# Gate sums kept plain until the branches read them, and several pieces of work in another order, in a one-core S5/attention/convolution layer

## The chip, the cores and the metric

One core of a Trainium2 chip runs the whole layer in one launch. The metric is the device time of one execution in microseconds (us). TensorE (PE) multiplies, VectorE (DVE), ScalarE (ACT) and GpSimd (POOL) do the elementwise work, SyncE (SP) issues nearly all transfers. Everything is float32; a matrix product is made of three matmuls on a split of each operand into a rounded part and a rest (hi·hi, hi·lo, lo·hi).

## What is computed

The layer, cut to what matters here (sequence 1024, width 1024, one layer):

```
proj = rms_norm(x, g1) @ w_in
u, q, k, v, cv, g = split(proj)                  # 512, 3x512, 512, 512, 1024, 3x1024 columns
y_s = GLU(gelu(S5(u)))                           # S5: 32 groups, a complex diagonal recurrence
y_a = dilated_attention(q, k, v) @ w_att_up      # three (window, dilation) patterns, merged by their log-sums
y_c = conformer_conv(cv) @ w_pw2                 # GLU, 31 taps per channel, layer norm, swish
gate = sigmoid(g + b_gate)                       # here as 0.5*(1+tanh(0.5*(g+b_gate)))
merged = gate[0]*y_s + gate[1]*y_a + gate[2]*y_c
x = x + merged @ w_out;  x = x + SwiGLU(rms_norm(x));  out = rms_norm(x)
```

## The kernel before

`run()` writes the program down stage by stage; a scheduler then orders each engine's instructions by their dependences and the places they were written at, and `tc.issue_after(x)` holds back what is written inside it until instruction x is issued. The engines then work strictly in that order. So where something is written, and in which queue a transfer stands, sets what waits behind it.

- **Start (0 to about 124 us).** `norm1` splits x into hi and lo; `conv_in(0)`, `project_v` and `project(0)` multiply it with columns of w_in (line L203 to L205 are the three matmuls of `gemms`). `conv(0)` is 31 steps on DVE into `cy` (L579). `s5_params` computes the recurrence's constants with many small DVE instructions, on tiles `sw`, `mr`, `pw`, `bb`; it is a generator in two parts, the first (some 100 instructions) written right after `project(0)`, the second in attention 0.
- **Attention (to about 547 us).** For each of 4 head pairs: `conv_in(hp+1)`, `attend0`, `attend1` (many small matmuls, a mask-and-minimum `soft` on DVE at L430, an exponential on ACT, transposes), `project(hp+1)`, `conv(hp)`. The evictions of `project` are on DVE (kn L417, q L417 and L424). The last head pair has no `project` of its own; instead `s5_tables` is written there: 44 DVE instructions twice over, which double a table `tab` of sines and cosines and store it.
- **Merge (547 to about 577 us).** `merge` weighs the results of `attend0` (first pattern, n0) and `attend1` (the other two, n1) (a chain PE, DVE, ACT, PE, ...: L515, L520, L525 to L534, L539, L546, L547) and stores the result (`od`, L550) from the SP queue.
- **Sides.** `project_u` multiplies for u (evicted by DVE to `uw`, L644). The gates use a seven-product scheme: two gates and two halves of the sequence take 7 products of half the depth instead of 8. Its right operands are seven sums of blocks of normed x: `early_sides` and `late_sides` load blocks `xb` (SP), scale them on DVE (`normed`, L662), add and split them (L675 to L693, L112). `first_products` runs the products that need early sides only: products 5 and 4 of gate pair 0, product 4 of pairs 1 and 2.
- **Gate stage (to about 924 us).** 12 pairs; `wino` runs the products in the order 1, 5, 2, 6, 4, 3, 7 through the PSUM banks u, y, v, z: products 1, 6 and 7 share bank u. After products 1, 5, 6, 4 ACT copies the bank to SBUF (`copy`, L710: m, y, n, z); after 2, 3, 7 DVE adds the other term (`add`, L716) and ACT takes the tanh in place (L717) and issues the store to DRAM `gd` (L718). Between products a `tick` hands out pieces of the eight S5 chunks (`s5`), one chunk every CHUNK = 8 products.
- **Branches (924 to 1156 us).** `gate(m, b)` loads a finished gate, two ahead of its use, from `gd`; DVE multiplies the branch's product by it. Then the output projection and the feed-forward part follow; the change does not touch them.

Of the kernel before, what the change touches and what calls it, by code (L numbers as in the profile page):

```python
# [9 lines left out]
F32 = mybir.dt.float32  # L10
# [19 lines left out]
CHUNK = 8  # L30
# [56 lines left out]
class Body:  # L87
# [158 lines left out]
    def run(self):  # L246
        tc, nc, V, A, G, PE = self.tc, self.nc, self.V, self.A, self.G, self.PE
        with ExitStack() as st:
# [8 lines left out]
            with pool("s5c") as self.sc, pool("h") as self.hp:  # L257
# [3 lines left out]
                with pool("at4") as self.ap4, pool("at1") as self.ap1, pool("at2") as self.ap2, pool("at3") as self.ap3, pool("at5") as self.ap5:  # L261
# [5 lines left out]
                    next(params)  # L267
                    for hp in range(HP):
                        if hp < HP - 1:
                            self.conv_in(hp + 1)  # L270
                        self.attend0(hp)
                        self.attend1(hp)
# [10 lines left out]
                early.close()  # L283
                self.bufs.update({"wraw": 6, "wsum": 3, "whi": 4, "wlo": 4, "t2": 8, "ct": 6, "l": 16, "r": 20})
                self.wp = enter(pool("w2", "right"))
                self.tp = right.enter_context(pool("t", "right"))
                with pool("xn") as self.xp, pool("uw") as self.up:
                    self.project_u()
                    begun = self.first_products()
                    for p in (1, 2, 3):  # L290
                        self.late_sides(p)
                with pool("s5") as self.sp:
                    self.gate_stage(begun)
# [109 lines left out]
    def project(self, hp):  # L403
# [15 lines left out]
        for a in (1, 2):  # L419
            q = self.ap2.tile([P, 4, 2, 2, 64], F32, tag=f"q{a}", name=f"q{a}")  # L420
            for h, ps in enumerate(self.gemm(win[4 + 4 * a + hp], self.hh, self.hl)):
                rb = perm(self.rb[:, 512 * h:512 * h + 512])
                for r in range(4):
                    V.tensor_tensor(out=q[:, r, :, :, 32 * h:32 * h + 32], in0=perm(ps)[:, r], in1=rb[:, r], op=ALU.mult)  # L424
            self.qkv.append(q)

    def soft(self, s, mask, c0, c1, pt, a, nm, den):

        w = self.ap2.tile([P, 320], F32, tag="sp", name="sp", bufs=2)
        self.V.tensor_tensor_reduce(out=w[:, c0:c1], in0=s[:, c0:c1], in1=mask[:, c0:c1], op0=ALU.add, op1=ALU.min,  # L430
                                    scale=1.0, scalar=3e38, accum_out=nm)
# [76 lines left out]
    def merge(self, half):  # L508
# [27 lines left out]
        for t in HALVES:  # L536
# [5 lines left out]
            for j in range(2):  # L542
# [7 lines left out]
                self.nc.sync.dma_start(out=self.od[hp][:, t], in_=self.n0[hp][:, t])  # L550
# [79 lines left out]
    def project_u(self):  # L630
        self.ud = self.dp.tile([L, 16, 32, NC], F32, name="ud")
        self.yd = self.dp.tile([BW, L, NC], F32, name="yd")
        self.kd = self.dp.tile([32, 16, KPAD + P], F32, name="kd")
        zero = self.tmp([P, 512])[:, 0:4 * KPAD].rearrange("p (a x) -> p a x", a=4)
        self.G.memset(zero, 0.0)
        self.nc.sync.dma_start(out=self.kd.rearrange("(a g) h x -> (g h) a x", a=4)[:, :, 0:KPAD], in_=zero)
        self.h1 = {}
        for ct in range(KB):
# [63 lines left out]
    def gate_pair(self, n, make, banks=None, only=PRODUCTS, kept=None):  # L702
# [26 lines left out]
    def first_products(self):  # L729

        self.gd = self.dp.tile([24, P, T], F32, name="gd")
        self.tick = lambda: None
        make = self.gate_left(0)
        begun = [(make, *self.gate_pair(0, make, only=(5, 4)), (1, 2, 6, 3, 7))]
# [681 lines left out]
```

## Time and profile before

| what | value |
|---|---|
| time, median of 3 runs (lowest to highest) | 1880.06 us (1879.17 to 1880.96) |
| the profiled execution's own time | 1877.27 us |
| its span in the trace | 1875.5 us |
| TensorE busy | 1777.2 us (95%) |
| mean granted TensorE clock | 0.963 of full speed |
| VectorE, ScalarE, GpSimd busy | 1303.8, 728.7, 865.9 us |

TensorE is busy for most of the span, but a matmul at a granted clock of 0.5 counts as busy for twice as long, so two things have to be read per stretch: the gaps of TensorE, and its clock.

### The profile page before, as it was taken

How to read it: one execution, taken by the hardware profiler on the slowest of the kernel's cores; microseconds unless marked ns; L12 is line 12 of the kernel's file. 1: busy time of each engine (PE TensorE's matmuls, PEld its weight loads, DVE VectorE, ACT ScalarE, POOL GpSimd, SP SyncE). 2: the span in 40 equal slices, each digit the busy share in tenths (PEclk: the TensorE clock that was granted, in tenths of full speed). 3: DMA queues.
4: the chain of work that ended last, by engine and by line, in shares of the span. 5: the costliest groups of instructions: out<-in, count | busy, mean ns of one | idle time of the engine just before them, and what ended most of it. 6: DMA issues, size and time to landing. Idle time of an engine off the chain costs nothing. (4 is left out here: it accounts for less than half of the span.)

```text
span 1875.5 us, 24385 instructions
## 1 busy us (share of the span) xinstructions
PE 1777.2 (95%) x8380; PEld 1392.3 (74%) x8380; DVE 1303.8 (70%) x2110; ACT 728.7 (39%) x1390; POOL 865.9 (46%) x707
## 2 busy tenths in 40 slices
PE   7989999999899689899999999989999999999997
PEld 5866675766657567788878878857888888778876
DVE  7964867746867987886467353698877776755556
ACT  5303314123141344445443233544555555433332
POOL 5622222222134665654325444665555445467671
PEclk9989999988888889999999999999999999999998
DMA  4430110210124534434752335313444444477752
GB/s 166 131 100 29 46 55 8 74 45 12 40 78 159 165 111 119 130 113 138 233 187 90 118 133 198 118 48 108 160 166 145 150 154 169 148 283 276 262 178 91
DMA packets 133516, 240.80 MB, mean 128 GB/s; under 512 B 13960, under 2 KB 55560, under 8 KB 133392
## 3 DMA queue, kind: packets, MB, share of 16 engines
q1 hardware_dynamic: 122576, 220.36, 34.9%
q10 hardware_dynamic: 10816, 18.88, 2.7%
q8 instruction: 66, 1.08, 0.2%
q14 instruction: 58, 0.48, 0.1%
HBM read 171.06 MB, written 68.12 MB: 128 GB/s over the span
## 5 line engine op out<-in xcount | busy, mean ns | idle before, releaser
L106 POOL TENSOR_TENSOR wlo<-wraw,whi 128x512 fp32r<-128x512 f32 x137 | 197.6, 1446 | 320.8 <-ACT whi L105 312.4
L112 POOL TENSOR_TENSOR wlo<-wsum,whi 128x512 fp32r<-128x512 f32 (+2 forms) x192 | 251.4, 1313 | 196.9 <-ACT whi L111 124.8
L112 POOL TENSOR_TENSOR wlo<-wraw,whi 128x512 fp32r<-128x512 f32 (+2 forms) x143 | 190.1, 1330 | 173.3 <-ACT whi L111 106.4
L167 PE MATMUL ps<-f,whi 128*128 128x512 f32 x616 | 241.7, 392 | 6.0 <-DVE f L112 4.0
L166 PE MATMUL ps<-f,whi 128*128 128x512 f32 x616 | 241.2, 392 | 5.3 <-ACT f L111 2.5
L105 ACT ACTIVATE whi<-wraw 128x512 fp32r<-128x512 f32 x135 | 84.6, 630 | 338.3 <-PE ps L204 225.7
L203 PE MATMUL ps<-hh,whi 128*128 128x512 f32 x448 | 186.6, 417 | 17.6 <-DVE kn L417 7.8
L204 PE MATMUL ps<-hl,whi 128*128 128x512 f32 x448 | 186.3, 417 | 4.1 <-DVE hl L349 4.1
L205 PE MATMUL ps<-hh,wlo 128*128 128x512 f32 x448 | 184.0, 411 | 0.0
L169 PE MATMUL ps<-f,wlo 128*128 128x512 f32 x616 | 165.5, 391 | 0.0
L166 PE MATMUL ps<-e,whi 128*128 128x512 f32 x336 | 138.8, 413 | 25.4 <-ACT n L710 10.0
L579 DVE SCALAR_TENSOR_TENSOR cy<-cx,hcw,cy 128x1024 f32<-128x1024 f32 x120 | 161.8, 1349 | 0.4
L111 ACT ACTIVATE whi<-wsum 128x512 fp32r<-128x512 f32 (+2 forms) x192 | 113.0, 592 | 119.2 <-PE ps L167 100.8
L167 PEld LDWEIGHTS ps<-f,whi 128*128 128x128 f32 x616 | 116.0, 188 | 33.9 <-DVE f L112 7.1
L166 PEld LDWEIGHTS ps<-f,whi 128*128 128x128 f32 x616 | 116.1, 188 | 32.0 <-ACT f L111 3.5
L167 PE MATMUL ps<-e,whi 128*128 128x512 f32 x336 | 135.7, 404 | 1.2 <-POOL e L112 1.2
L169 PEld LDWEIGHTS ps<-f,wlo 128*128 128x128 f32 x616 | 116.2, 189 | 24.2
L203 PEld LDWEIGHTS ps<-hh,whi 128*128 128x128 f32 x448 | 88.9, 198 | 42.8 <-issue 15.9
L111 ACT ACTIVATE whi<-wraw 128x512 fp32r<-128x512 f32 (+2 forms) x143 | 84.6, 592 | 87.0 <-PE ps L167 58.7
L166 PE MATMUL ps<-g,whi 128*128 128x512 f32 x280 | 109.5, 391 | 2.8 <-DMA g<-ad 2.7
L112 DVE TENSOR_TENSOR g<-ct,g 128x512 fp32r<-128x512 f32 x79 | 81.7, 1040 | 40.6 <-ACT g L111 40.4
L167 PE MATMUL ps<-g,whi 128*128 128x512 f32 x280 | 109.0, 389 | 0.0
(309 smaller groups left out, 3900.7 us busy)
## 6 DMA issues: line engine op xcount, KB each, us to landing
ad<-g SPq DMA_DIRECT2D x65, 512.0 KB
g<-ad SPq DMA_DIRECT2D x65, 512.0 KB
wraw<-in_win SPq DMA_DIRECT2D x122, 256.0 KB
wraw<-in_wffi SPq DMA_DIRECT2D x96, 256.0 KB
gate<-gd SPq DMA_DIRECT2D x24, 512.0 KB
wraw<-in_wffo SPq DMA_DIRECT2D x48, 192.0 KB
xb<-in_xt SPq DMA_DIRECT2D x32, 256.0 KB
wraw<-in_wout SPq DMA_DIRECT2D x32, 256.0 KB
```

The lines of the kernel that those rows point to most:

```text
L105: eng.tensor_copy(hi, raw) if eng else self.A.activation(hi, raw, AF.Copy)
L106: self.G.tensor_tensor(out=lo, in0=raw, in1=hi.bitcast(F32), op=ALU.subtract)
L111: self.A.activation(hi, src, AF.Copy)
L112: eng.tensor_tensor(out=lo, in0=src, in1=hi.bitcast(F32), op=ALU.subtract)
L166: PE.matmul(o, hi[:, k, :], xh, start=first and k == 0, stop=False, skip_group_check=not first)
L167: PE.matmul(o, hi[:, k, :], xl, start=False, stop=False, skip_group_check=not first)
L169: self.mm = PE.matmul(o, lo[:, k, :], xh, start=False, stop=k == n - 1, skip_group_check=not first).ins
L203: self.PE.matmul(o, hi[:, k, :], xh[k0 + k][:, t], start=first, stop=False)
L204: self.PE.matmul(o, hi[:, k, :], xl[k0 + k][:, t], start=False, stop=False)
L205: self.mm = self.PE.matmul(o, lo[:, k, :], xh[k0 + k][:, t], start=False, stop=last).ins
L579: V.scalar_tensor_tensor(out=cy, in0=cx[:, j:j + T], scalar=self.hcw[:, ct * TAPS + j:ct * TAPS + j + 1], in1=cy, op0=ALU.mult, op1=ALU.add)
```

## The change

What it does, by its parts:

1. After the DVE sums of the gate stage nothing follows on ACT. The plain sum is put on a list (`late`) and stored to `gd` from the SP queue two products later; `gate(m, b)` takes the tanh over 128x1024 after loading it.
2. `first_products` runs product 4 of pairs 1 to 5 (EARLY = 6), stores their copies to DRAM `zd` from SP, and `next_pair` loads them back.
3. The S5 chunks come every 7 products instead of 8, the first two pieces at products 9 and 12 instead of 4 and 7.
4. Part 1 of `s5_params` is written in attention 0, after the last q eviction of `project(0)`; part 2 stays where it was. The zero fill of `kd` moves to its end.
5. `s5_tables` may start only after the second `soft` of the last head pair's `attend0`.
6. The first three u weights are loaded ahead of the tables, the other five at the top of `project_u`.
7. The pool `at5` (v, kn, tables) is opened ahead of `at4`, so that the later `xb` tiles come to lie on other memory than n0 and n1 of the merge.
8. `merge` stores `od` from the POOL queue instead of SP's (4 stores in each of 2 merges).

The diff, cut to its core:

```diff
-CHUNK = 8
+CHUNK = 7
+EARLY = 6
...
-                with pool("at4") as self.ap4, pool("at1") as self.ap1, pool("at2") as self.ap2, pool("at3") as self.ap3, pool("at5") as self.ap5:
+                with pool("at5") as self.ap5, pool("at4") as self.ap4, pool("at1") as self.ap1, pool("at2") as self.ap2, pool("at3") as self.ap3:
...
                     params = self.s5_params()
-                    next(params)
+                    evicted = self.evicted
...
                         self.attend0(hp)
+                        soft = self.softs[1]
+                        if hp == 0:
+                            with tc.issue_after(evicted):
+                                next(params)
                         self.attend1(hp)
...
-                            self.s5_tables()
+                            self.first_u = [self.weights(self.i["win"][k // 2][:, 4 * (k % 2):4 * (k % 2) + 4], 4) for k in range(3)]
+                            with tc.issue_after(soft):
+                                self.s5_tables()
...
-                self.nc.sync.dma_start(out=self.od[hp][:, t], in_=self.n0[hp][:, t])
+                self.nc.gpsimd.dma_start(out=self.od[hp][:, t], in_=self.n0[hp][:, t])
...
+        self.ahead += [self.weights(self.i["win"][k // 2][:, 4 * (k % 2):4 * (k % 2) + 4], 4) for k in range(3, 8)]
...
                 V.tensor_tensor(out=x, in0=banks[b], in1=x, op=ALU.add)
-                A.activation(x, x, AF.Tanh, scale=0.5, bias=self.hbg[:, m:m + 1])
-                self.nc.scalar.dma_start(out=self.gd[m, :, HALVES[h]], in_=x)
+                self.late.append((self.ticks + 2, self.gd[m, :, HALVES[h]], x))
...
-        for n in (1, 2):
-            begun.append((None, *self.gate_pair(n, self.gate_left(n), only=(4,)), (1, 5, 2, 6, 3, 7)))
+        for n in range(1, EARLY):
+            r = self.gate_pair(n, self.gate_left(n), only=(4,))[1]
+            self.nc.sync.dma_start(out=self.zd[n], in_=r["z"])
...
+    def tick(self):
+
+        self.ticks += 1
+        while self.late and self.late[0][0] <= self.ticks:
+            _, dst, x = self.late.pop(0)
+            self.nc.sync.dma_start(out=dst, in_=x)
+        for part in self.parts.pop(self.ticks, ()):
+            with self.tc.issue_after(self.mm):
+                next(part)
...
+        elif n < EARLY:
+            z = self.tmp([P, 512], "z")
+            self.nc.sync.dma_start(out=z, in_=self.zd[n])
+            self.gate_pair(n, self.gate_left(n), None, (1, 5, 2, 6, 3, 7), {"z": z})
...
-        put(4, 0)
-        put(7, 0)
+        put(9, 0)
+        put(12, 0)
...
     def gate(self, m, b):
         t = self.tp.tile([P, 2, 512], F32, tag="t1", name="gate", bufs=4).rearrange("p a b -> p (a b)")
         self.nc.sync.dma_start(out=t, in_=self.gd[8 * b + m])
+        self.A.activation(t, t, AF.Tanh, scale=0.5, bias=self.hbg[:, 8 * b + m:8 * b + m + 1])
         return t
```

**DVE around the first key eviction.** `sw` is the parameters' scratch tile, `cy` the convolution's sum, `kn` the first eviction of `project(0)`. Before:

```order
L793 TENSOR_SCALAR sw_995<-sw_995 128x16
L846 TENSOR_SCALAR sw_995<-sw_995 128x16
L789 TENSOR_SCALAR sw_995<-sw_995 128x16
L790 TENSOR_SCALAR sw_995<-sw_995 128x16
L792 SCALAR_TENSOR_TENSOR sw_995<-sw_995 128x16 x3
L793 TENSOR_SCALAR sw_995<-sw_995 128x16
L417 SCALAR_TENSOR_TENSOR kn<-ps,rb 128x512 x2
L479 COPY kp<-kn 128x1024
```

In the changed kernel (lines have moved by 9 or 10: kn is L426):

```order
L576 TENSOR_TENSOR t_393<-ps,rb 128x512
L579 SCALAR_TENSOR_TENSOR t_393<-t_393,ps 128x512
L586 TENSOR_SCALAR cy<-cx_274,hcw,vecs 128x1024
L589 SCALAR_TENSOR_TENSOR cy<-cx_274,hcw,cy 128x1024 x30
L426 SCALAR_TENSOR_TENSOR kn<-ps,rb 128x512 x2
L489 COPY kp<-kn 128x1024
```

The parameter instructions that stood between the convolution and kn are gone from there.

**PE at the end of the last head pair's attention.** L203 to L205 before, L204 to L206 now, are the matmuls for u (`hh`, `hl` are the split normed x); L515 and L520 before, L525 and L530 now, are the first transposes of the merge. Before:

```order
L502 MATMUL ps<-ptT,v 64x128 x4
L438 MATMUL ps<-con,p 128x128 x4
L515 MATMUL ps<-con,stat 8x128 x8
L502 MATMUL ps<-ptT,v 64x128 x4
L438 MATMUL ps<-con,p 128x128 x4
L520 MATMUL ps<-con,r_4336 128x8 x8
L502 MATMUL ps<-ptT,v 64x128 x4
L539 MATMUL ps<-con,e 8x128 x4
L203 MATMUL ps<-hh_121,whi 128x512
L204 MATMUL ps<-hl_129,whi 128x512
L203 MATMUL ps<-hh_121,whi 128x512
```

In the changed kernel:

```order
L525 MATMUL ps<-con,stat 8x128 x4
L205 MATMUL ps<-hl_130,whi 128x512
L512 MATMUL ps<-ptT,v 64x128 x4
L448 MATMUL ps<-con,p 128x128
L525 MATMUL ps<-con,stat 8x128 x4
L206 MATMUL ps<-hh_122,wlo 128x512
L448 MATMUL ps<-con,p 128x128 x3
L204 MATMUL ps<-hh_123,whi 128x512
L530 MATMUL ps<-con,r_4358 128x8 x8
L205 MATMUL ps<-hl_131,whi 128x512
L206 MATMUL ps<-hh_123,wlo 128x512
L204 MATMUL ps<-hh_124,whi 128x512
```

The matmuls for u now stand ahead of and between the merge's transposes, where before the first of them came behind L539.

**ACT in the gate stage.** Copies of the banks (L710 before, L717 now), splits of the weights (`whi`), and before also tanh (L717) and stores (L718). Before:

```order
L710 ACTIVATE m<-ps 128x512
L111 ACTIVATE whi<-wsum 128x512
L111 ACTIVATE whi<-wraw 128x512
L946 ACTIVATE hs<-ca 64x2x128 x2
L717 ACTIVATE m<-m,hbg 128x512
L946 ACTIVATE hs<-ca 64x2x128 x2
L718 DMA gd<-m 128x512
L710 ACTIVATE n<-ps 128x512
L111 ACTIVATE whi<-wsum 128x512
L111 ACTIVATE whi<-wraw 128x512
L973 ACTIVATE gt<-ps 128x512
L717 ACTIVATE n<-n,hbg 128x512
```

In the changed kernel:

```order
L717 ACTIVATE m<-ps 128x512
L112 ACTIVATE whi<-wsum 128x512
L717 ACTIVATE y<-ps 128x512
L112 ACTIVATE whi<-wsum 128x512
L112 ACTIVATE whi<-wraw 128x512
L717 ACTIVATE n<-ps 128x512
L112 ACTIVATE whi<-wsum 128x512
L717 ACTIVATE z<-ps 128x512
L1054 ACTIVATE yg<-ps 128x512
L112 ACTIVATE whi<-wraw 128x512
L112 ACTIVATE whi<-wsum 128x512
```

No instruction is left on ACT that needs a DVE sum of the gates.

## Rows read from the trace of the kernel before

**Rows 1.** The page, busy time: each engine's busy us, share, instructions.

```profile
PE 1777.2 (95%) x8380; PEld 1392.3 (74%) x8380; DVE 1303.8 (70%) x2110; ACT 728.7 (39%) x1390; POOL 865.9 (46%) x707
```

**Rows 2.** Busy time by stretch (`us, PE busy (x) PEld busy (x) DVE busy (x) ACT busy (x) POOL busy (x), PEclk, DMA share, GB/s`).

```profile
459.00:503.00 44.00, 38.17 (x182) 30.57 (x181) 43.38 (x89) 3.10 (x6) 6.95 (x5) 0.95 0.10 36
503.00:547.00 44.00, 42.87 (x310) 25.82 (x310) 30.59 (x118) 24.39 (x76) 7.81 (x17) 0.89 0.09 37
547.00:579.00 32.00, 28.84 (x76) 16.01 (x77) 10.59 (x23) 4.84 (x9) 11.74 (x9) 0.57 0.41 129
579.00:640.00 61.00, 49.37 (x206) 39.41 (x205) 59.89 (x62) 19.70 (x34) 32.62 (x21) 0.93 0.56 177
640.00:700.00 60.00, 48.68 (x199) 37.36 (x200) 53.38 (x74) 22.58 (x43) 42.55 (x40) 0.84 0.37 124
700.00:924.00 224.00, 215.74 (x1116) 176.92 (x1116) 161.17 (x268) 109.71 (x195) 116.94 (x103) 0.99 0.44 136
924.00:1156.00 232.00, 229.98 (x1021) 188.39 (x1020) 122.82 (x174) 79.77 (x127) 100.58 (x74) 1.00 0.46 156
```

**Rows 3.** TensorE's timeline at 117 us: start, length, line, operation, [idle before <- releaser].

```profile
117.35 0.76 PE L203 MATMUL ps<-hh,whi 128*128 128x512 f32 x1 [7.76 <-DVE kn L417]
...
123.45 0.39 PE L205 MATMUL ps<-hh,wlo 128*128 128x512 f32 x1
```

**Rows 4.** Busy time of the `sw` tile's instructions alone, 43 to 117 us.

```profile
43.00:117.00 74.00, 32.51 (x99) 0.00 (x0) 0.97 0.39 120
```

**Rows 5.** Busy time by stretch, 182 to 215 us.

```profile
182.00:215.00 33.00, 31.74 (x226) 19.38 (x225) 23.22 (x50) 14.12 (x41) 10.46 (x17) 1.00 0.03 9
```

**Rows 6.** What TensorE waited for, 100 to 300 us: total, times, longest.

```profile
PE ps L203 <- DVE q L424: 2.5, 1, 2.5
```

**Rows 7.** TensorE's timeline where the last head pair's attention starts.

```profile
502.91 1.43 PE L459 MATMUL ps<-kn,q 64*128 64x256 f32 x4 [5.83 <-DVE stat L430]
```

**Rows 8.** Busy time of the `tab` tiles' instructions alone, in two stretches.

```profile
464.00:504.00 40.00, 14.19 (x44) 0.94 0.11 40
504.00:543.00 39.00, 11.49 (x44) 0.89 0.07 28
```

**Rows 9.** Groups of VectorE instructions, 545 to 650 us: busy, mean ns, idle before.

```profile
L662 DVE SCALAR_TENSOR_TENSOR xb<-xb,vecs,rb 128x512 f32<-128x512 f32 x32 | 34.5, 1113 | 0.7 <-DMA xb<-in_xt 0.7
...
L548 DVE TENSOR_TENSOR n<-n,ps 128x512 f32<-128x512 f32 x8 | 5.5, 688 | 12.1 <-PE ps L547 12.1
```

**Rows 10.** VectorE's timeline at 581 us.

```profile
581.15 0.75 DVE L662 SCALAR_TENSOR_TENSOR xb<-xb,vecs,rb 128x512 f32<-128x512 f32 x1 [0.71 <-DMA xb<-in_xt]
...
587.44 1.78 DVE L662 SCALAR_TENSOR_TENSOR xb<-xb,vecs,rb 128x512 f32<-128x512 f32 x1
```

**Rows 11.** GpSimd's timeline at 587 us.

```profile
586.99 1.68 POOL L112 TENSOR_TENSOR e<-xb,e 128x512 fp32r<-128x512 f32 x1 [3.22 <-ACT e L111]
```

**Rows 12.** What TensorE waited for in the gate stage, 600 to 925 us.

```profile
PE ps L166 <- ACT n L710: 10.0, 4, 5.0
...
PE ps L166 <- ACT m L710: 4.5, 3, 2.5
PE ps L166 <- ACT z L710: 3.9, 1, 3.9
```

**Rows 13.** Busy time by stretch, after the longest wait of the gate stage.

```profile
761.70:765.00 3.30, 3.30 (x8) 2.63 (x9) 1.23 (x1) 1.45 (x3) 3.27 (x3) 0.50 0.60 213
```

**Rows 14.** Line L717, the tanh of the gate sums: durations, and idle time before them.

```profile
L717 ACT ACTIVATE n<-n,hbg x12: 722/724/727, 668.8 to 921.9; 128x512 f32<-128x512 f32 x12
...
  DVE m L716: 51.0, 11
```

**Rows 15.** ScalarE's timeline at 759 us.

```profile
759.31 0.72 ACT L717 ACTIVATE m<-m,hbg 128x512 f32<-128x512 f32 x1 [8.04 <-DVE m L716]
...
761.05 0.58 ACT L710 ACTIVATE n<-ps 128x512 f32<-128x512 f32 x1
```

**Rows 16.** Groups of ScalarE instructions in the branches, 924 to 1156 us.

```profile
L105 ACT ACTIVATE whi<-wraw 128x512 fp32r<-128x512 f32 x49 | 30.5, 628 | 71.3 <-PE ps L204 41.2 <-issue 15.3 <-DMA cn<-cd 4.8
```

More of the change, by code (lines that the diff above doesn't have):

```diff
@@ L283, in run @@
                 early.close()
+                self.ahead = self.first_u
                 self.bufs.update({"wraw": 6, "wsum": 3, "whi": 4, "wlo": 4, "t2": 8, "ct": 6, "l": 16, "r": 20})
@@ L288, in run @@
                     self.project_u()
-                    begun = self.first_products()
+                    self.first_products()
                     for p in (1, 2, 3):
@@ L731, in first_products, with next_pair @@
         self.gd = self.dp.tile([24, P, T], F32, name="gd")
-        self.tick = lambda: None
+        self.zd = self.dp.tile([EARLY, P, 512], F32, name="zd")
+        self.late, self.ticks, self.parts = [], 0, {}
         make = self.gate_left(0)
-        begun = [(make, *self.gate_pair(0, make, only=(5, 4)), (1, 2, 6, 3, 7))]
-        for n in (1, 2):
-            begun.append((None, *self.gate_pair(n, self.gate_left(n), only=(4,)), (1, 5, 2, 6, 3, 7)))
+        self.begun = make, *self.gate_pair(0, make, only=(5, 4))
+        for n in range(1, EARLY):
+            r = self.gate_pair(n, self.gate_left(n), only=(4,))[1]
+            self.nc.sync.dma_start(out=self.zd[n], in_=r["z"])
         for p in (1, 2, 6):
             make(p, keep=True)
-        return begun
+    def tick(self):
[6 more added lines that the diff above has]
+                next(part)
+    def next_pair(self):
+        n = self.todo.pop(0)
+        if n == 0:
+            make, banks, r = self.begun
+            self.gate_pair(0, make, banks, (1, 2, 6, 3, 7), r)
+        elif n < EARLY:
+            z = self.tmp([P, 512], "z")
+            self.nc.sync.dma_start(out=z, in_=self.zd[n])
+            self.gate_pair(n, self.gate_left(n), None, (1, 5, 2, 6, 3, 7), {"z": z})
+        else:
+            self.gate_pair(n, self.gate_left(n))
     def toeplitz(self, g):
@@ L744, in toeplitz, with gate_stage @@
         return bass.AP(tensor=src.tensor, offset=src.offset, ap=[[16, L], [KPAD + P, 16], [1, P]])
-    def gate_stage(self, begun):
+    def gate_stage(self):
         n = 16 // NJ
-        parts = [self.s5(e) for e in range(n)]
-        at = {}
+        chunks = [self.s5(e) for e in range(n)]
         def put(t, e):
             if e < n:
-                at.setdefault(t, []).append(e)
-        put(4, 0)
-        put(7, 0)
+                self.parts.setdefault(self.ticks + t, []).append(chunks[e])
+        put(9, 0)
+        put(12, 0)
         for e in range(n):
-            t = 7 + CHUNK * e
+            t = 12 + CHUNK * e
             put(t + 3, e + 1)
@@ L764, in gate_stage @@
         for e in (0, 1):
-            next(parts[e])
-        self.ticks = 0
-        def tick():
-            self.ticks += 1
-            for e in at.pop(self.ticks, ()):
-                with self.tc.issue_after(self.mm):
-                    next(parts[e])
-        self.tick = tick
+            next(chunks[e])
         self.todo = list(range(len(GATES)))
-        while at:
-            g = self.todo.pop(0)
-            make, banks, r, only = begun[g] if g < len(begun) else (None, None, None, PRODUCTS)
-            self.gate_pair(g, make or self.gate_left(g), banks or None, only, r)
+        while self.parts:
+            self.next_pair()
     def last_gates(self):
-        self.tick = lambda: None
-        for g in self.todo:
-            self.gate_pair(g, self.gate_left(g))
+        while self.todo:
+            self.next_pair()
+        self.ticks += 2
+        self.tick()
     def reduce_angle(self, a, w, n):
```

18 lines of the change are left out of this document (10 added, 8 removed).

## The prediction

> **What bounds the kernel now.** I read the page first: TensorE is busy for 1777.2 of 1875.5 us, VectorE for 1303.8 [rows 1]. So at most about 98 us are gaps of TensorE; the rest of what can be won is time in which it ran at the lower clock and counted as busy. The table by stretches shows where both lie [rows 2]. From 924 us on TensorE is busy for 229.98 of 232 us at full clock, 1021 matmuls, so 0.225 us each. In the gate stage (700 to 924) it misses 8 us; from 579 to 640 it misses 11.6 and from 640 to 700 11.3 us, with VectorE full in the first of these (59.89 of 61). The merge (547 to 579) runs at a granted clock of 0.57 with VectorE used for 10.59 of 32 us. From 459 to 503 VectorE is full (43.38 of 44) and TensorE is not (38.17). Last I read what ends the waits at each such place.
>
> **The start.** TensorE waits 7.76 us for kn, and then its matmuls start 0.436 us apart (14 of them from 117.35 to 123.45) instead of 0.225: 7.76 + 14 x 0.21 = 10.7 us [rows 3]. The clock had fallen behind the wait to the lower of its two levels (1.2 of 2.4 GHz). VectorE spent those microseconds on part 1 of the parameters, whose instructions cost 32.51 us in all up to there [rows 4]; the order shows them gone from ahead of kn. Gain 10.7. But they come back in the next stage, where VectorE has 33.0 - 23.22 = 9.8 us free between 182 and 215 us [rows 5], and where the evictions of the next projection are late already: TensorE waits 2.5 us for q at about 257 [rows 6]. Part 2 can slip behind that eviction, as nobody needs it before the gate stage; some 40 small instructions more than before stay ahead of it, about 7 us. With the free time I take 3 us of loss; none if all fits, 7 if none does. Net **-7.7** (ends -10.7 and -3.6).
>
> **Tables and the last attention.** It starts 5.83 us late behind VectorE's work [rows 7], and its stretch has a mean clock of 0.89, so 0.11 x 44 = 4.8 us more. One half of the tables (14.19 us, 44 instructions) lay ahead of that point; the other half (11.49) in the attention itself [rows 8]. Now all of it comes after the second `soft`. VectorE has 13.4 us free in 503 to 547 [rows 2], but attention is a chain through VectorE, so I let half of the 14.19 lengthen it: -5.8 - 4.8 + 7.1 = **-3.5** (ends -10.6, all hidden; +3.6, all in the chain).
>
> **Merge.** VectorE waits 12.1 us for the merge's own matmuls (L548) [rows 9], at about half clock. The order puts matmuls for u between the steps of the chain, so TensorE stays busy and the clock up: half of the 12.1. The blocks `xb` no longer lie on n0 and n1, so they land earlier and VectorE can do some of the 32 scalings (1.1 us each [rows 9]) in its idle time; three of them, 3 us. **-9** (ends -3, those three alone; -21.4, all that VectorE is idle there). The stores of `od` move from SP to POOL; nothing reads them before the branches' operands are built, and SP's loads no longer stand behind them: nothing.
>
> **Three more early products.** 12 matmuls each, 3 x 12 x 0.225 = 8.2 us leave the gate stage and go into TensorE's 11.6 idle us of 579 to 640. Each also brings a split on GpSimd into a stretch where VectorE is full, and the two slow each other: the same scaling took 0.75 us alone and 1.78 beside a GpSimd instruction [rows 10, 11]. Three such encounters cost 3 x 1.03 = 3.1. **-5.1** (ends -8.2; +3.1 if the products find no idle time). The Trainium skill has a rule on this that speaks against the change ("SBUF — State Buffer", section "Who interferes with whom"): a VectorE instruction with two SBUF inputs and a GpSimd instruction that reads SBUF exclude each other for the whole instruction. By that rule each encounter could cost up to the whole 1.68 us of the GpSimd instruction [rows 11], so 5.0 instead of 3.1 and a sum 1.9 us higher; the trace agrees that they exclude each other and shows less than the whole. The stores of z are only 5 on SP, but each waits for its product's copy and holds back two or three of the last 11 `xb` loads behind it; I count that in the +3.1 end.
>
> **Gate stage.** Product 7 goes into the bank that the copy n has to empty. ACT issues in order, and a tanh that waits for a late VectorE sum stands ahead of that copy: at 759 us the tanh of m waited 8.04 us, and n was copied right behind it [rows 15]. TensorE waits 10.0 us for n in all, 5.0 the longest time, 4.5 for m and 3.9 for z [rows 12]; after the longest one 3.3 us ran at half clock [rows 13], 1.65 lost. Without tanh in that queue the n waits and this slow stretch go: **-11.7** (ends -5.0, only the longest; -16.2, the m waits too). 48 tanh of 0.72 us [rows 14] leave an engine that had room, as do their store issues: nothing by themselves. The later chunks move the same S5 work: nothing.
>
> **Branches.** 24 tanh of twice the width, by 2 x 0.72 = 1.44 us each an estimate of 35 us, go to ACT, which is busy for 79.77 of 232 there [rows 2] and waits 41.2 us for TensorE before its weight splits (L105) [rows 16]. The cover is that slack; a tanh that waits for its load would hold the splits behind it. Two tanh in series at the start would cost **+2** (ends 0 and +8).
>
> **Sum.** -7.7 - 3.5 - 9 - 5.1 - 11.7 + 2 = -35.0 against the profiled execution's 1877.3: 1842.3. The median of the runs shown is 1880.06, 2.8 above it, so 1845.
>
> **Rivals.**
>
> 1. *The waits only move: VectorE is the bound from 124 to 640.* For it: VectorE is full from 459 to 503 and from 579 to 640 [rows 2], and no VectorE work is removed there. Against it: it is idle for 35 us in between. Then each term stands at or near its poor end: -3.6 + 3.6 - 3 + 0 - 10 + 2 = -11, so 1869.
> 2. *The gate stage keeps its waits.* VectorE's sums are late because of S5 steps ahead of them; with ACT freed, TensorE would wait for VectorE itself to empty bank v. Against it: the bank is needed again only a pair later. The term of 11.7 falls away: 1857.
> 3. *Slower: the wait moves from ACT's queue to SP's.* The stores of the sums now stand among SP's weight loads. If a sum is later than two products (24 x 0.225 = 5.4 us) and the loads ahead are used up, the next weights wait as the tanh did: 51.0 us in 11 waits for m alone [rows 14], 4.6 each. Over 12 pairs that is 55.6 us, and the gate stage's gain is gone: -23.3 + 55.6 = +32.3, so 1912. From 27 of the 55.6 us on the kernel is slower by over 0.2%. Against it: weights are loaded several ahead, and the average wait is below 5.4.
> 4. *No effect:* gains and losses cancel at the poor ends: about 1880.
> 5. *Better:* the good ends of start, attention and merge come together: below 1830.
>
> **How the numbers follow.** Forecast as summed 0.48, with a range of its own of 1830 to 1858; rival 1 0.20, rival 2 0.13, rival 3 0.07, rival 4 0.05, better 0.07. The range 1818 to 1872 takes in the forecast, rivals 1 and 2 and most of the better case. The bound for "the same" is 0.2%, 3.8 us, about what a measurement of this kernel can tell from no change. Faster: 0.48 + 0.20 + 0.13 + 0.07 = 0.88; same 0.05; slower 0.07.
>
> **What would show it.** Right: no wait for kn at about 107 us; the last attention begins right behind its projection; u matmuls inside the merge at a clock near 1; the gate stage shorter by about three products and no wait for n behind a tanh; the branches as long as before. Wrong: a wait for q at 250 us that has grown by 5 or more, an attention longer by over 7 us, TensorE waiting for VectorE in the sides for longer than before, weight loads in the gate stage that land late behind stores, or TensorE waiting for `whi` in the branches.

## The result and the profile after

The changed kernel takes 1833.68 us (median of 4 runs, 1828.21 to 1834.54) where the kernel before, beside it, takes 1880.51. The ratio is 0.974, 95% interval 0.9715 to 0.9766: 47 us less by the medians. Forecast were 1845 (35 less) and a range of 1818 to 1872. The profiled execution has a span of 1832.3 us, 43.2 less.

The page's first rows of the changed kernel, to be laid beside [rows 1]:

```profile
span 1832.3 us, 24390 instructions
## 1 busy us (share of the span) xinstructions
PE 1758.9 (96%) x8380; PEld 1381.8 (75%) x8380; DVE 1314.8 (72%) x2110; ACT 726.8 (40%) x1366; POOL 878.0 (48%) x715
```

TensorE executes the same 8380 matmuls and is busy for 18.3 us less: that part of the gain is mainly clock, not work. The other 25 us are gaps that closed.

To place the difference I cut the span at six events: the beginning of attention 0, of the strided half of attention 1 (`attend1(1)`), of the last attention, the last matmul of the second merge, the last gate product, and the last matmul of the last large product (some small matmuls of the final norm follow, 9.1 to 9.6 us in every kernel). Lengths of the stretches in us, read from the timelines of TensorE to about 0.2 us:

| kernel | A: to attention 0 | B: to attend1(1) | C: to attention 3 | D: to the merge's end | E: to the last gate product | F: to the last large product's end |
|---|---|---|---|---|---|---|
| before | 164.1 | 135.8 | 196.9 | 75.8 | 351.3 | 935.3 |
| changed | 154.3 | 142.2 | 191.5 | 68.5 | 325.3 | 933.7 |
| difference | -9.8 | +6.4 | -5.4 | -7.3 | -26.0 | -1.6 |

Not all of E is waiting that went: TensorE starts 1534 matmuls in it before and 1481 now. The 53 others, some 12 us at 0.225 us each, are matmuls for u that now run in the last attention and in the merge.

Busy time by stretch in the changed kernel (columns as in [rows 2]): attention 3, merge, the rest of the u matmuls, sides, gate stage, and behind it as long a stretch as the last one of [rows 2].

```profile
488.00:532.00 44.00, 43.53 (x315) 26.04 (x315) 34.14 (x140) 23.18 (x71) 7.74 (x15) 1.00 0.06 25
532.00:557.00 25.00, 23.84 (x115) 15.31 (x114) 19.46 (x52) 4.93 (x11) 6.42 (x7) 1.00 0.44 144
557.00:592.00 35.00, 29.95 (x121) 23.91 (x121) 34.87 (x33) 8.68 (x15) 23.71 (x17) 0.90 0.53 172
592.00:700.00 108.00, 88.42 (x402) 67.63 (x401) 95.50 (x117) 44.65 (x81) 71.42 (x61) 0.97 0.53 168
700.00:882.00 182.00, 182.00 (x963) 150.73 (x962) 151.79 (x254) 74.27 (x130) 103.18 (x91) 1.00 0.53 159
882.00:1114.00 232.00, 231.24 (x1029) 189.97 (x1028) 124.59 (x174) 103.23 (x150) 100.43 (x75) 1.00 0.46 155
```

From 700 us on TensorE has next to no gap: it is busy for 182.00 of 182 us in the gate stage and 231.24 of 232 behind it. The merge, at a clock of 0.57 before [rows 2], runs at full clock in this execution; kernel 7 below, with the same order on TensorE, has 11.2 us of it at half clock. What is left lies between 592 and 700 us: 19.6 us without a matmul, VectorE used for 95.50 of 108.

What TensorE waits for from 585 to 900 us, to be laid beside [rows 12]:

```profile
PE ps L167 <- ACT z L717: 7.0, 4, 2.7
PE ps L168 <- POOL e L113: 4.2, 5, 1.3
PE ps L167 <- ACT m L717: 3.8, 2, 3.4
```

The wait for n, 10.0 us before, is gone from the list. So is the second wait in the list before, which [rows 12] pass over: a gate product at 628 us that waited for an eviction of u to `uw`.

```profile
PE ps L166 <- DVE uw L644: 6.5, 1, 6.5
```

The wait for z has grown: five products 4 follow one another through one bank.

### The profile page after: what moved, and what is told of

It is laid out like the page before. It is cut to its first block, busy times and chain, and to the rows that moved or that the text cites. A ratio compares the mean times of both kernels' runs of the same rounds, so it can differ in the third digit from the quotient of the medians.

```text
span 1832.3 us, 24390 instructions
## 1 busy us (share of the span) xinstructions
PE 1758.9 (96%) x8380; PEld 1381.8 (75%) x8380; DVE 1314.8 (72%) x2110; ACT 726.8 (40%) x1366; POOL 878.0 (48%) x715
## 5 line engine op out<-in xcount | busy, mean ns | idle before, releaser
L113 POOL TENSOR_TENSOR wlo<-wsum,whi 128x512 fp32r<-128x512 f32 (+2 forms) x192 | 259.6, 1357 | 177.9 <-ACT whi L112 85.1
L204 PE MATMUL ps<-hh,whi 128*128 128x512 f32 x448 | 183.7, 411 | 14.1 <-ACT whi L106 6.6
L205 PE MATMUL ps<-hl,whi 128*128 128x512 f32 x448 | 182.1, 407 | 4.2 <-DVE hl L358 4.2
L206 PE MATMUL ps<-hh,wlo 128*128 128x512 f32 x448 | 181.6, 407 | 2.6 <-POOL wlo L107 2.6
L589 DVE SCALAR_TENSOR_TENSOR cy<-cx,hcw,cy 128x1024 f32<-128x1024 f32 x120 | 179.5, 1496 | 1.7
L167 PE MATMUL ps<-e,whi 128*128 128x512 f32 x336 | 135.0, 402 | 14.7 <-ACT z L717 7.0
L168 PE MATMUL ps<-e,whi 128*128 128x512 f32 x336 | 132.9, 395 | 4.9 <-POOL e L113 4.2
L204 PEld LDWEIGHTS ps<-hh,whi 128*128 128x128 f32 x448 | 87.1, 194 | 37.7 <-issue 9.0
L113 DVE TENSOR_TENSOR g<-ct,g 128x512 fp32r<-128x512 f32 x79 | 78.0, 993 | 42.7 <-ACT g L112 42.5
```

Of the source, the lines that this page charges most:

```text
L113: eng.tensor_tensor(out=lo, in0=src, in1=hi.bitcast(F32), op=ALU.subtract)
L167: PE.matmul(o, hi[:, k, :], xh, start=first and k == 0, stop=False, skip_group_check=not first)
L168: PE.matmul(o, hi[:, k, :], xl, start=False, stop=False, skip_group_check=not first)
L204: self.PE.matmul(o, hi[:, k, :], xh[k0 + k][:, t], start=first, stop=False)
L205: self.PE.matmul(o, hi[:, k, :], xl[k0 + k][:, t], start=False, stop=False)
L206: self.mm = self.PE.matmul(o, lo[:, k, :], xh[k0 + k][:, t], start=False, stop=last).ins
```

## The experiments

Each kernel is the changed one with one edit, run beside the kernel before. A reading of the stretches stands behind each; all of them are gathered in a table at the end of the section.

**1. Parameters put back behind `project(0)`.**

```diff
                     params = self.s5_params()
-                    evicted = self.evicted
+                    next(params)
...
-                        if hp == 0:
-                            with tc.issue_after(evicted):
-                                next(params)
```

> The changed kernel with part 1 of the parameters put back right behind project(0). Theory: the start gained 9.8 us (attention 0 begins at 154.1 instead of 163.9 us) and lost 6.5 of it again because the parameters lie ahead of the q evictions and the tanh chain of conv_in at 250 to 272 us; so undoing it costs only 3 us (about 1837) and the wait for kn of 7 to 8 us is back while the waits at 250 and 270 us go. Rival: the 6.5 us came from a clock that fell at 272 us by itself; then undoing costs the whole 10 us (about 1844).

1845.79 us (1844.33 to 1853.43), ratio 0.9842 (0.9816 to 0.9868): 12 us slower than the changed kernel. What TensorE waits for from 100 to 300 us, this kernel first, then the changed one:

```profile
PE ps L204 <- DVE kn L423: 7.6, 1, 7.6
PE ps L204 <- DVE q L430: 2.5, 1, 2.5
```

```profile
PE ps L204 <- DVE sw L810: 2.4, 1, 2.4
PE ps L204 <- DVE t L576: 2.1, 1, 2.1
```

The wait for kn is back, and stretch A is 9.3 us longer. As expected by the theory, a wait (t, 2.1 us) goes at the far end. But stretch B did not become shorter, 144.9 us against 142.2, because 20.5 us of it ran at half clock, from 203 us on. Neither account had that; the total is 2 us above the rival's number, and its mechanism, a clock that falls apart from the parameters, is at least part of it: in the changed kernel, too, 13.6 us of stretch B ran at half clock, 3.4 before, which is 5.1 of the 6.4 us that B grew by. A fall of the clock between 197 and 203 us stands in the profiles of all thirteen changed kernels, this one with the parameters put back included, and not in that of the kernel before; what sets it off stays open.

**2. Tanh of the gate sums back on ScalarE in the gate stage.**

```diff
-                self.late.append((self.ticks + 2, self.gd[m, :, HALVES[h]], x))
+                A.activation(x, x, AF.Tanh, scale=0.5, bias=self.hbg[:, m:m + 1])
+                self.nc.scalar.dma_start(out=self.gd[m, :, HALVES[h]], in_=x)
...
-        self.A.activation(t, t, AF.Tanh, scale=0.5, bias=self.hbg[:, 8 * b + m:8 * b + m + 1])
         return t
```

> The changed kernel with tanh and stores of the gate sums back on ScalarE in the gate stage and none in the branches. Theory: the tanh that waits for a late VectorE sum holds back the copy n; TensorE waits for n again, 8 to 12 us in 650 to 890, and the time is about 1845. Rival: the gate stage got shorter by the three products and the later S5 pieces alone; then the time stays within 3 us of 1834.

1853.79 us (1851.78 to 1856.83), ratio 0.9874 (0.9851 to 0.9898): 20 us slower, more than expected. TensorE's waits from 585 to 900 us in this kernel:

```profile
PE ps L167 <- ACT m L717: 10.9, 7, 3.3
PE ps L167 <- ACT n L717: 10.5, 5, 4.7
PE ps L167 <- ACT z L717: 7.0, 4, 2.6
```

The longest of them on ScalarE's timeline, then on TensorE's:

```profile
682.92 0.72 ACT L724 ACTIVATE m<-m,hbg 128x512 f32<-128x512 f32 x1 [7.29 <-DVE m L723]
...
684.65 0.58 ACT L717 ACTIVATE n<-ps 128x512 f32<-128x512 f32 x1
```

```profile
685.28 0.80 PE L167 MATMUL ps<-e,whi 128*128 128x512 f32 x1 [4.68 <-ACT n L717]
```

A tanh waits 7.29 us for its sum, the copy n stands behind it, TensorE waits 4.68 for the copy. Against the changed kernel the listed waits are 17.6 us more (n 10.5, m 7.1), and others are fewer: all gaps of TensorE in stretch E are 10.8 us more. E, with 1480 matmuls (1481 in the changed kernel), is 21.8 us longer; the other half of that is clock, 36.0 us at half clock against 13.7. Two of the falls, at 684 and 731 us, lie behind such waits. The rival falls. The edit also puts the 48 stores back on ScalarE's queue, 0.33 us each to issue, which this run doesn't part from the tanh.

**3. Tanh on ScalarE in the gate stage, two products behind its sum.**

```diff
-                self.late.append((self.ticks + 2, self.gd[m, :, HALVES[h]], x))
+                self.late.append((self.ticks + 2, self.gd[m, :, HALVES[h]], x, m))
...
-            _, dst, x = self.late.pop(0)
+            _, dst, x, m = self.late.pop(0)
+            self.A.activation(x, x, AF.Tanh, scale=0.5, bias=self.hbg[:, m:m + 1])
...
-        self.A.activation(t, t, AF.Tanh, scale=0.5, bias=self.hbg[:, 8 * b + m:8 * b + m + 1])
         return t
```

> The changed kernel with the tanh of the gate sums back on ScalarE in the gate stage, but written two products behind its sum, the store behind it from SP; none in the branches. Theory: not the 35 us of ScalarE work cost the 20 us, but the wait of a tanh for its sum ahead of the copies; two products later the sum is there, so the time stays at 1831 to 1838. Rival: ScalarE's work itself, its place among splits and copies, is what costs; then 1845 to 1854 as with the tanh right behind the sum.

1847.12 us (1844.55 to 1849.43), ratio 0.9823 (0.9809 to 0.9838). Between the two: 14.6 us of the 21.8 in stretch E stay. ScalarE's waits in this kernel, its timeline at 682 us, and TensorE's waits:

```profile
ACT m L753 <- DVE m L723: 49.6, 9, 7.9
```

```profile
682.36 0.72 ACT L753 ACTIVATE m<-m,hbg 128x512 f32<-128x512 f32 x1 [7.90 <-DVE m L723]
...
683.50 0.58 ACT L717 ACTIVATE n<-ps 128x512 f32<-128x512 f32 x1
```

```profile
PE ps L167 <- ACT m L717: 11.0, 6, 3.4
PE ps L167 <- ACT n L717: 6.0, 3, 2.8
```

The premise failed. In the program's text the tanh of m now stands behind the copies n and z; the scheduler put it back ahead of copy n in 11 of the 12 pairs, as the order on ScalarE shows (L717 are copies, L753 the tanh):

```
L717 ACTIVATE y<-ps 128x512
L112 ACTIVATE whi<-wsum 128x512
L753 ACTIVATE m<-m,hbg 128x512
L112 ACTIVATE whi<-wraw 128x512
L717 ACTIVATE n<-ps 128x512
```

So ScalarE waits 49.6 us for the sums of m, about as in the kernel before [rows 14], and copy n waits behind it. A tanh that stands behind the copies was thus not tried, and the run doesn't part the waiting from the tanh's work, 48 x 0.72 = 35 us, nor either from the stores, which SP issues here; how the 21.8 us divide between them stays open. Laid over ScalarE's timeline, the 21.4 us that TensorE waits for copies m and n in kernel 2 hold some 4 us of a tanh's wait for its sum, 4 of tanh and 6 of the copies themselves; the rest is other work that had piled up in the queue. What the two runs show is that with the tanh in that queue 13 to 20 us of the gain are gone.

**4. Tables free to start before the last attention.**

```diff
-                            with tc.issue_after(soft):
-                                self.s5_tables()
+                            self.s5_tables()
```

> The changed kernel with the tables free to start before the last attention. Theory: the first half of the tables goes back ahead of attention 3, which starts 5 us later and is shorter by about as much: within 3 us of 1834. Rival: the wait of 5.83 us and the half clock behind it come back and nothing is returned: about 1843.

1843.77 us (1841.22 to 1847.92), ratio 0.9817 (0.9794 to 0.984): 10 us slower. The rival is right. Attention 3's start on TensorE's timeline:

```profile
497.11 1.22 PE L468 MATMUL ps<-kn,q 64*128 64x256 f32 x2 [6.74 <-DVE stat L439]
```

Without the hold the tables run ahead of the attention's steps on VectorE, TensorE waits 6.74 us and then runs at half clock for 13.7 us; stretch D is 80.4 us long against 68.5. What the tables cost inside the attention is small: from the first strided step to the end of attention 3 it is 32.4 us in the changed kernel and 33.0 here (27.8 before). Nor are the tables what makes it longer than before: in kernels 11 and 12, which hold them back too but run no matmul for u inside the attention (the changed kernel runs 14 in this part of it), it is 28.4 us.

**5. Three early products instead of six.**

```diff
-EARLY = 6
+EARLY = 3
```

> The changed kernel with EARLY = 3. Theory: three products (36 matmuls of 0.225 us, 8.2 us) go from idle TensorE time in the sides back into the gate stage: about 1842. Rival: the early products delay the sides by their splits on GpSimd and by the stores that hold back loads, so that most of the 8 us is given back: about 1836 or less.

1832.86 us (1829.95 to 1841.42), ratio 0.9769 (0.9744 to 0.9795): no difference from the changed kernel that the intervals show; stretch E is 326.3 against 325.3 (C is shorter and D longer by the clock). The rival is right. Busy time from 593 to 645 us, here and in the changed kernel:

```profile
593.00:645.00 52.00, 39.74 (x141) 28.14 (x142) 49.20 (x52) 22.66 (x41) 37.52 (x28) 0.90 0.54 181
```

```profile
593.00:645.00 52.00, 36.07 (x137) 25.91 (x136) 42.23 (x43) 22.53 (x41) 32.07 (x22) 0.96 0.64 206
```

With six early products TensorE executes no more matmuls in these 52 us than with three (137 and 141), while VectorE is busy for less (42.23 us and 49.20). The early products did not fill idle time; they took the place of others.

**6. Early products and parameters further: EARLY = 9, and part 2 of the parameters one head pair later (7: the latter alone).**

```diff
-                        if hp == 0:
+                        if hp < 2:
                             with tc.issue_after(evicted):
                                 next(params)
                         self.attend1(hp)
-                        if hp == 0:
-                            with tc.issue_after(self.exp_last):
-                                next(params)
                         if hp < HP - 1:
                             self.project(hp + 1)
+                            evicted = self.evicted
...
-EARLY = 6
+EARLY = 9
```

> As n_late2, with EARLY = 9, three more early products. Theory of the early products as a filler: TensorE still waits some 18 us between 593 and 645 us in the changed kernel, so three more products gain again, up to 8 us against n_late2. Rival: product 4 always goes into bank z, and TensorE waits for the copy of z each time (7.0 us in the changed kernel for five), the splits on GpSimd delay the sides; then 0 to 4 us slower than n_late2.

> The changed kernel with part 2 of the parameters one head pair later, behind the last q eviction of project(1). Theory: the 5 us that attention 1 starts late in the changed kernel (27.3 us from the first matmul of attend0(1) to attend1(1), 22.2 before) are VectorE time of part 2 ahead of the tanh chain of conv_in and the soft steps; they go, and the head pair behind has room for it: 1828 to 1830. Rival: the same 18 us of small instructions delay the next head pair instead: 1833.

With both 1835.55 us (1830.81 to 1841.59), ratio 0.9762 (0.974 to 0.9785); with the parameters alone 1832.46 (1825.96 to 1833.77), 0.9739 (0.9722 to 0.9756). Nine early products are 1.1 us longer than six in stretch E: the rival again. The parameters' edit told nothing: stretch B is 141.9 against 142.2, and the same waits are there (sw 2.4, t 2.1 us), because part 2 may start right behind the last q eviction of `project(1)`, and that is where it had run already (256 to 270 us in the changed kernel). Its theory was not tested, and as TensorE's order is the changed kernel's, instruction for instruction, this run is nearly a second measurement of it (VectorE's order differs, up to 260 us).

**8. `od` stores back on SP's queue.**

```diff
-                self.nc.gpsimd.dma_start(out=self.od[hp][:, t], in_=self.n0[hp][:, t])
+                self.nc.sync.dma_start(out=self.od[hp][:, t], in_=self.n0[hp][:, t])
```

> The changed kernel with the od stores back on SP's queue. Theory: each store waits for GpSimd's sum and holds back the loads behind it on SP (in the kernel before SP waited 18.7 us for the sums in the first merge), but no engine was waiting for those loads then; in the second merge the blocks xb stand behind it, so 0 to 5 us are lost: 1834 to 1839. Rival: the stores on GpSimd's queue cost GpSimd time in the sides, and undoing gains 2 to 4 us.

1829.08 us (1825.9 to 1830.58), ratio 0.9735 (0.9714 to 0.9757), an interval that overlaps the changed kernel's. Its profiled execution is 8.1 us shorter than the changed kernel's, and 6.6 of that is in stretch C, where the two kernels' TensorE instructions stand in the same order. Attention 2 in the changed kernel and here, to the same event:

```profile
411.30:454.60 43.30, 42.65 (x248) 25.74 (x247) 26.73 (x54) 13.91 (x40) 10.46 (x17) 0.80 0.02 7
```

```profile
409.70:446.40 36.70, 35.45 (x248) 21.83 (x248) 26.60 (x54) 13.82 (x40) 10.43 (x17) 1.00 0.03 8
```

The same 248 matmuls take 43.3 us at a mean clock of 0.80 and 36.7 at 1.00. From attention 3 to the end of stretch F both kernels take the same time within 0.1 us, 1327.4. The median is 4.6 us below the changed kernel's, outside what the theory allowed and nearer to the rival; but the intervals overlap, and the largest difference by stretch, C's, goes with its clock. The queue of these stores makes no difference that can be seen.

**9 to 11. The S5 places, the pool order, the u weights.**

```diff
-CHUNK = 7
+CHUNK = 8
...
-        put(9, 0)
-        put(12, 0)
+        put(4, 0)
+        put(7, 0)
```

> The changed kernel with the S5 pieces at products 4, 7 and then every 8 as before. Theory: with no tanh behind the sums a late VectorE step delays only its own bank, so the places of the pieces hardly matter: within 3 us of 1834. Rival: the earlier first pieces bring GpSimd's and VectorE's S5 work back into the sides, where TensorE waits for VectorE; then 4 to 8 us slower, with waits for gm again.

1834.39 us (1831.69 to 1839.8), ratio 0.9769 (0.9746 to 0.9793). In the total no difference; in stretch E 4.5 us longer, with one wait of the rival's kind:

```profile
PE ps L994 <- POOL gm L950: 9.3, 1, 9.3
```

In the pool's undoing `at5` is opened last, as before:

> The changed kernel with pool at5 opened last again, so that the blocks xb lie on n0 and n1 of the merge. Theory: the scalings start only after the merge has released n0 and n1, VectorE stays idle in the merge as before, and 5 to 9 us come back: about 1841. Rival: the matmuls for u alone shortened the merge; then within 2 us of 1834.

1834.18 us (1833.26 to 1836.99), ratio 0.9771 (0.9748 to 0.9793): the rival; stretch D is 68.4 us as with the change, E 4.4 longer. The u weights without their early loads:

```diff
-                            self.first_u = [self.weights(self.i["win"][k // 2][:, 4 * (k % 2):4 * (k % 2) + 4], 4) for k in range(3)]
...
-        self.ahead += [self.weights(self.i["win"][k // 2][:, 4 * (k % 2):4 * (k % 2) + 4], 4) for k in range(3, 8)]
```

> The changed kernel without the early loads of the u weights (first_u and the list at the top of project_u). From the start of attention 3 to the last u matmul the changed kernel takes 103.5 us, the kernel before 117.3. Theory: it is the weights at hand that let the u matmuls fill the attention and the merge; undoing it lengthens that stretch by 8 to 14 us, time 1842 to 1848. Rival: the blocks and VectorE set that stretch; then within 3 us of 1834.

1831.26 us (1829.63 to 1839.66), ratio 0.9763 (0.9738 to 0.9788): the rival again; D 68.9, E 4.2 longer. From the start of attention 3 to the last matmul for u, the stretch that the theory named, it takes 104.3 us where the changed kernel takes 104.2. What the early loads do can still be seen. Without them no matmul for u runs in the last attention (23 in the changed kernel), which is 5.8 us shorter, and the wait for `uw` of the kernel before is back (535 to 900 us):

```profile
PE ps L167 <- DVE uw L648: 8.9, 3, 6.6
```

In the total the two come out about even.

**12. Three parts alone: parameters, tables, tanh.** The five other undoings together.

> The changed kernel with only three of its parts: parameters later, tables held back, tanh in the branches; the other five (od queue, early products, S5 places, pool order, u weights) as before. Theory: these three carry the change (undone one by one they cost 12, 10 and 20 us, 42 of 46.8), so the time is 1833 to 1841. Rival: each of the five others is worth 4 to 7 us in the stretch behind the start of the last attention, and was hidden by the clock's chance falls in the totals; then 1848 to 1858.

1840.38 us (1831.02 to 1842.23), ratio 0.9772 (0.975 to 0.9794). The theory holds: three parts give some 40 of the 47 us by the medians. The profiled execution took 1832.61 us, 7.8 below the median, and is within 0.7 us of the changed kernel's up to the end of E; so the 7 us between the two medians, whose intervals overlap, are not placed. The other five parts, each worth nothing that its total shows, together shift the work: D is 6.7 us shorter without them, as no u matmul stands in it, and E 13.2 longer, with this wait:

```profile
PE ps L167 <- DVE uw L648: 5.6, 1, 5.6
```

The stretches of all kernels, in us, and how much of C and D ran at half clock:

| kernel | A | B | C | half clock in C | D | half clock in D | E | F |
|---|---|---|---|---|---|---|---|---|
| before | 164.1 | 135.8 | 196.9 | 27.3 | 75.8 | 36.2 | 351.3 | 935.3 |
| changed | 154.3 | 142.2 | 191.5 | 17.1 | 68.5 | 0 | 325.3 | 933.7 |
| 1 parameters back | 163.6 | 144.9 | 192.5 | 17.1 | 68.7 | 1.3 | 324.4 | 933.6 |
| 2 tanh back | 154.1 | 141.4 | 185.0 | 0 | 71.6 | 8.4 | 347.1 | 936.0 |
| 3 tanh two products later | 154.4 | 142.2 | 185.0 | 0 | 71.6 | 8.3 | 339.9 | 933.8 |
| 4 tables free | 153.1 | 141.2 | 193.9 | 20.5 | 80.4 | 17.1 | 323.6 | 933.3 |
| 5 EARLY = 3 | 154.0 | 142.1 | 185.0 | 0 | 74.3 | 14.6 | 326.3 | 932.5 |
| 6 EARLY = 9, part 2 later | 153.2 | 141.3 | 191.5 | 17.1 | 68.5 | 0 | 327.0 | 935.6 |
| 7 part 2 later | 154.3 | 141.9 | 185.0 | 0 | 74.3 | 14.6 | 325.9 | 933.8 |
| 8 od on SP | 153.5 | 141.4 | 184.9 | 0 | 71.5 | 8.2 | 322.7 | 933.2 |
| 9 S5 places | 154.5 | 142.3 | 191.5 | 17.1 | 68.5 | 0 | 329.8 | 935.0 |
| 10 pool order | 154.4 | 141.5 | 191.5 | 17.1 | 68.4 | 1.3 | 329.7 | 932.8 |
| 11 u weights | 154.6 | 142.1 | 185.0 | 0 | 68.9 | 6.8 | 329.5 | 933.1 |
| 12 three parts alone | 154.0 | 141.8 | 185.0 | 0 | 61.8 | 15.6 | 338.5 | 932.6 |

No version tried beats the changed kernel by more than the intervals: the fastest, with od on SP, has 0.9735 (0.9714 to 0.9757).

## Why the prediction was right, point by point

The direction and the size were right, 35 us forecast and 47 measured, and the parts that carry the gain, start, tables and gate stage, do so by the mechanisms named. The terms were not right in size, and that the sum came as near as it did is in part luck: by the undoings those three were some 19 us too small, and the merge and the early products, 14.1 us of the forecast, give nothing that an undoing clearly shows:

- **Start, -7.7 (ends -10.7 and -3.6).** Undone, it costs 12 us. The gain itself is as worked out: 9.8 us in stretch A. The loss behind it is there too, but of the 6.4 us that B grew by 5.1 are clock; the waits at 250 and 270 us, 4.5 in all against 2.5 before, are 2 us more. The 12 is what the undoing costs in these executions, a longer fall of the clock in attention 0 included.
- **Tables, -3.5 (ends -10.6 and +3.6).** Undone, 10 us: the good end. The wait of 5.83 us [rows 7] and the half clock went. The 7.1 us that I took for tables inside the attention were not paid: its strided half did grow by 4.6 us (27.8 to 32.4), but by the matmuls for u that now run in it. Without them, tables held back alike, it takes 28.4 (kernels 11 and 12), 0.6 more than before.
- **Merge, -9.** From the end of attention 3 to the end of the merge 4.8 us were gained (23.9 to 19.1), then 6.4 more up to the last u matmul. The 4.8 are in part luck: kernel 7, with the same order on TensorE, takes 23.4 us there with 11.2 at half clock. Nor does a clock kept up by matmuls for u make the merge short, as I had it: kernel 12 has none in it, 15.6 us at half clock, and takes 18.2. What the order does is to run 49 of these matmuls inside the merge, 19 before. The causes that I gave, weights at hand and blocks on other memory, cost nothing in the total when undone one at a time, 4 us each in stretch E. Which of them matters for the total stays open.
- **Early products, -5.1.** The step that failed: "3 x 12 x 0.225 = 8.2 us leave the gate stage and go into TensorE's 11.6 idle us". (The product is 8.1.) Measured: nothing, with three, six or nine. The idle time is not free room: VectorE, which scales and adds the sides, is busy for 95.50 of 108 us there, and a product more needs its bank emptied by ScalarE (7.0 us of waits for z). The encounters of VectorE and GpSimd that I counted belong to this, as a part of it that I priced and set against a gain that wasn't there.
- **Gate stage, -11.7 (ends -5.0 and -16.2).** Mis-sized: 20 us by experiment 2. The term that was too small is the clock, 1.65 us taken from one slow stretch: the gaps that the tanh brings back are 10.8 us, near the 10.0 forecast, and 22.3 us more at half clock cost another 11. The gaps are not those of n alone: the tanh of z and y stand ahead of the next pair's copy m, and of kernel 2's 10.9 us of waits for m all but 1.8 lie behind the first tanh. How much of the clock goes with the tanh is less sure, as E has from 13.7 to 29.4 us at half clock in the kernels without it. The wait of 6.5 us for `uw` at 628 us stood in no term; it is back where the early loads of the u weights are undone (8.9 us in kernel 11, 5.6 in 12). Rival 2 (the sums themselves hold TensorE) fell: the list after shows 1.4 us of waits for a sum (m 0.9, n 0.5), and no gap after 700 us. So did rival 3: from 700 us to the end of the gate stage TensorE waited for no weights.
- **Branches, +2.** Nothing lost, stretch F is 1.6 us shorter. The cover held, though not without waits: the tanh takes 1.15 us rather than 1.44, and ScalarE waited 16.4 us for the gates' loads ahead of it, while TensorE was busy for 231.24 of 232 us there (229.98 before [rows 2]). The tanh in the changed kernel, and its idle time:

```profile
L1064 ACT ACTIVATE gate<-gate,hbg x24: 1122/1152/1156, 879.5 to 1049.5; 128x1024 f32<-128x1024 f32 x24
...
  DMA gate<-gd: 16.4, 11
```

- **Not in the sum:** 5.4 us between the profiled executions in stretch C. They come with 10.2 us less at half clock (27.3 and 17.1), which is worth 5.1 us, and this fall differs between executions of one order (last section); so part of the 43.2 us between the two profiled executions is luck. Rival 1, that the waits only move, shows in B and in the early products; its price of -11 held the gate stage at -10, twice its own poor end.

## What to carry to other kernels

Work that can be done later should not stand among the instructions that free banks, least of all where it waits for a slower engine: 48 tanh of 0.72 us, on an engine used for under half the time, cost 20 us with their stores and the waits ahead of them, and moved to a stage where that engine has slack they cost nothing that shows. Look for such places by asking what is queued behind each wait of an engine that looks idle. Before filling idle time of an engine with more work, ask who made it idle; if the filler needs that engine too, it can move work and gain nothing, as three, six and nine early products did here.

## What was not expected of the hardware

**The same order of instructions, 6.5 us apart.** Stretch C takes 185.0 us in one group of kernels (2, 3, 5, 7, 8, 11, 12) and 191.5 in another (the changed one, 6, 9, 10), with 17.1 us at a granted clock of 0.5 in the second (the two rows of experiment 8). Kernel 7 and the changed one, each in one execution, have the same order on TensorE throughout and lie in different groups. So do kernel 3 and the changed one, whose TensorE, VectorE, ScalarE and GpSimd all have the same order up to 636 us. Ahead of the fall at 428.8 us TensorE did the same in both; the changed kernel first, then kernel 3:

```profile
384.00:411.00 27.00, 26.83 (x157) 17.83 (x156) 16.15 (x43) 12.03 (x37) 6.03 (x5) 1.00 0.10 30
```

```profile
384.00:411.00 27.00, 26.83 (x157) 17.86 (x155) 16.15 (x43) 12.03 (x37) 6.11 (x5) 1.00 0.08 30
```

As the order does not decide it, it seems to belong to the execution. Much of it comes back in D: the kernels of the first group have 6.8 to 15.6 us at half clock there, those of the second 0 to 1.3. In C and D together kernels 7 and 3 are 0.7 and 3.4 us shorter than the changed one. So single parts are judged by stretch, not by the total alone, and C and D are read together.

**A short VectorE instruction can take as long as the GpSimd instruction it meets.** VectorE's timeline in the changed kernel at 227 and 256 us, then GpSimd's:

```profile
227.30 0.16 DVE L849 TENSOR_TENSOR pw<-mr,sw 128x16 f32<-128x16 f32 x1
...
256.24 1.22 DVE L849 TENSOR_TENSOR pw<-mr,sw 128x16 f32<-128x16 f32 x1
```

```profile
256.14 1.29 POOL L107 TENSOR_TENSOR wlo<-wraw,whi 128x512 fp32r<-128x512 f32 x1 [8.98 <-ACT whi L106]
```

The 16-column instruction lasts 1.22 us beside GpSimd's 1.29, and both end within 0.03 us of each other; the same instruction took 0.16 us at 227 us, with GpSimd idle. The scaling of [rows 10, 11] began 0.45 us after GpSimd's instruction, so 1.23 of its 1.68 us were left, and it lost 1.03. The Trainium skill ("SBUF — State Buffer", "Who interferes with whom") has the pair of ports that the two engines share as an exclusive lock, held for the whole instruction by whichever issues first, while the other is blocked. Both traces agree with it nearly in full; the prediction read less than the whole out of the second because it counted GpSimd's instruction from its start.

**Stores issued by GpSimd.** Each od store kept GpSimd for 0.56 us where SP needed 0.32; they landed after 2.3 to 7.6 us, and the trace shows nothing that waited for them:

```profile
L560 POOL DMA_DIRECT2D od<-n x8: 559/559/712, 373.3 to 560.4; - x8
...
DMA to landing us min/median/max: 2.3/2.5/7.6
```

```profile
L550 SPq DMA_DIRECT2D od<-n x8: 320/326/327, 376.3 to 575.1; - x8
```
